# Two of four token tiles take their layer-norm sums on ScalarE, and half of the last stores leave from its queue

## The chip, the cores and the metric

The kernel runs on one core of a Trainium2 chip. The metric is the device time of one execution in microseconds (us), as the median of several runs. The engines are TensorE (PE in the profile; PEld is its weight load), VectorE (DVE), ScalarE (ACT), GpSimd (POOL) and SyncE (SP), which only issues DMAs. Each engine works through its own queue in the order in which the program was laid out, and waits on semaphores for the others.

## The reference

Two transformer blocks run one after the other on 512 tokens of width 1024, in float32. The first has a hybrid mixer, a cross-attention over 256 memory tokens and a mixture of 16 experts; the second is modulated by a conditioning vector and has a Hyena mixer (FFT-like long convolutions) and an expert-choice mixture of 16 experts. What matters here is the layer norm that stands between the stages:

```python
def layer_norm(x, g, b):
    xf = x.astype(jnp.float32)
    mu = xf.mean(-1, keepdims=True)
    var = jnp.square(xf - mu).mean(-1, keepdims=True)
    return ((xf - mu) * lax.rsqrt(var + LN_EPS) * g + b).astype(x.dtype)
...
x = _ln_affine(DEEPNORM_ALPHA_2 * x + (1.0 + m_l[2]) * yl, ln_g[i, 0], ln_b[i, 0])
hl = _modulate(x, m_l[3], m_l[4])
x = _ln_affine(DEEPNORM_ALPHA_2 * x + (1.0 + m_l[5]) * _expert_choice_moe(hl, moe_router[i], moe_w1[i], moe_w3[i], moe_w2[i]),
               ln_g[i, 1], ln_b[i, 1])
```

`_modulate` is a second layer norm (without its own g and b) that is scaled and shifted by modulation rows, so a token tile goes through two norms in a row before it enters the next stage. The last norm gives the output.

## The kernel before, in words

The 512 tokens lie as four **tiles** of 128 tokens (partitions) by 1024 features. The text calls them tile 0 to tile 3; `xr[:, j]` is the residual stream of tile j. The norms are computed at these three places, which the change touches:

- **First norms** (`combine`, L1282 to L1305, at 758 to 808 us): after the first expert mixture. Per tile one add (L1283), a norm in place on `xr` with the position table `pe` added (`ln_affine`), then a norm into a separate tile `mo` (`ln_modulate`). PE transposes `mo` (L360), ACT copies the result out as the high half `hlh` (L235) and DVE subtracts for the low half `hll` (L236). Between them stand ACT's copies of `pe` (L1265) and the splitting of the first Hyena weights (`wh`, L228 on ACT and L231 on DVE). PE starts the first Hyena products on tiles 0 and 1 (`hyena_first`) while tiles 2 and 3 are still in their norms, and finishes them when those are there.
- **Second norms** (`route2`, L1549 to L1555, at 1081 to 1129 us): after the Hyena mixer. Per tile two halves of the product are scaled (L1552) and added (L1553), then normed in place on `xr`, then normed into `hl`, from which the router's affinities come. Tile 0's second norm is spread already: its sums are on ACT (`ln_stats_act`, L327 and L330), its affine part on ACT (L350) and POOL (L351, L352).
- **Last norms** (`moe2`, L1767 to L1782, at 2074 us to the end): on the sums in PSUM (`pcb`), in halves of 512. Tiles 0 and 1 get their affine part on ACT (L1776), DVE (L1777) and POOL (L1778), tiles 2 and 3 on DVE alone (L1780, L1781). Eight stores of 256 KB go out from SP's queue (L1782).

On DVE the statistics are two `bn_stats` on halves of 512 (L316), one `bn_aggr` (L318) and an add of epsilon (L320). Then POOL takes the power -0.5 (`ly`, L308), while DVE does (r - mu) * g (L339), which doesn't need `ly`. When `ly` is there, DVE does the second step, times `ly` plus b (L340).

The order of instructions on each engine is set by the tile framework's scheduler from the order of the calls, the data dependencies and the `issue_after` marks, and is fixed when the program is built. Between the second and the last norms lies the second expert mixture: SP streams all its weights (some 190 loads of 2 MB) through eight slots of SBUF, from 1079 us on, and PE works them off.

Of the kernel before, what the change touches and what calls it, by code (L numbers as in the profile page):

```python
# [13 lines left out]
AF = mybir.ActivationFunctionType  # L14
ALU = mybir.AluOpType
# [4 lines left out]
P = 128  # L20
S = 512
D = 1024
# [181 lines left out]
class Builder:  # L204
# [129 lines left out]

    def ln_affine(self, r, eps, g, b, out=None):
        vec = self.nc.vector
        mu, rs = self.ln_stats(r, eps)
        out = r if out is None else out
        vec.scalar_tensor_tensor(out, r, mu, g, op0=ALU.subtract, op1=ALU.mult)  # L339
        return vec.scalar_tensor_tensor(out, out, rs, b, op0=ALU.mult, op1=ALU.add)  # L340

    def ln_modulate(self, r, sc, sh, out, spread=False):

        if not spread:
            return self.ln_affine(r, 1e-6, sc, sh, out=out)
        nc = self.nc
        mu, rs = self.ln_stats_act(r, 1e-6, out)
        nm = self.small([P, 1], "nmr")
        nc.vector.scalar_tensor_tensor(nm, mu, -1.0, rs, op0=ALU.mult, op1=ALU.mult)
        nc.scalar.activation(out, r, AF.Identity, bias=nm, scale=rs)  # L350
        nc.gpsimd.tensor_tensor(out, out, sc, op=ALU.mult)  # L351
        return nc.gpsimd.tensor_tensor(out, out, sh, op=ALU.add)  # L352
# [896 lines left out]
    def combine(self, xr, ig, tables):  # L1249
# [32 lines left out]
        def norms(j):  # L1282
            vec.tensor_tensor(xr[:, j], xr[:, j], ys[:, j], op=ALU.add)  # L1283
            last.append(self.ln_affine(xr[:, j], 1e-5, g, pe[:, j]))
            mo = self.wide(name="mo")
            last.append(self.ln_modulate(xr[:, j], sc, sh, mo))
            return mo
# [228 lines left out]
    def route2(self, xr, z2, w):  # L1516
# [32 lines left out]
        def norms(j):  # L1549
            for n in range(2):  # L1550
                c = slice(n * 512, (n + 1) * 512)
                tt(hl[:, j, c], pbs[j][n], g2[:, c], op=ALU.mult)  # L1552
                tt(xr[:, j, c], xr[:, j, c], hl[:, j, c], op=ALU.add)  # L1553
            self.ln_affine(xr[:, j], 1e-5, g, b)
            self.ln_modulate(xr[:, j], sc, sh, hl[:, j], j == 0)  # L1555

# [64 lines left out]
    def moe2(self, xr, hl, sv, aff):  # L1621
# [145 lines left out]
        for j in range(4):  # L1767
            mu, rs = self.ln_stats(pbs[j], 1e-5)
            if j < 2:
                nm = self.small([P, 1], "nmr")  # L1770
                vec.scalar_tensor_tensor(nm, mu, -1.0, rs, op0=ALU.mult, op1=ALU.mult)
            for h in range(2):
                c = slice(h * 512, (h + 1) * 512)
                o = xr[:, j, c]
                if j < 2:
                    act.activation(o, pbs[j][h], AF.Identity, bias=nm, scale=rs)  # L1776
                    tt(o, o, gb[0][:, c], op=ALU.mult)  # L1777
                    pool.tensor_tensor(o, o, gb[1][:, c], op=ALU.add)  # L1778
                else:
                    vec.scalar_tensor_tensor(o, pbs[j][h], mu, gb[0][:, c], op0=ALU.subtract, op1=ALU.mult)  # L1780
                    vec.scalar_tensor_tensor(o, o, rs, gb[1][:, c], op0=ALU.mult, op1=ALU.add)  # L1781
                nc.sync.dma_start(self.out[:, j, c], o)  # L1782

# [17 lines left out]
```

## Time and profile before

| | us |
|---|---|
| runs | 2095.79, 2084.8, 2096.02; median 2095.79 |
| profiled execution, time | 2096.14 |
| its span in the profile | 2094.4 |

| engine | busy us | share of the span |
|---|---|---|
| PE | 1854.0 | 89% |
| DVE | 944.2 | 45% |
| ACT | 536.8 | 26% |
| POOL | 186.3 | 9% |

The shares are means over stages with different limits. In the first half DVE and ACT are busy at 3 to 8 tenths, in the second half, the last expert mixture, at 0 to 2 tenths, while the DMA engines move 427 GB/s. A row of the timeline gives start, duration, engine, line, operation, output and input tiles with their shapes, and in brackets how long the engine stood idle before it and what ended that. SPq and ACTq are the DMA issues of those queues.

### The profile page before, as it was taken

To read this page: it belongs to the slowest core of one execution; us is meant where nothing else is said; L and a number is where in the kernel's file an instruction comes from. 1 tells how busy PE (TensorE), PEld (TensorE's weight loads), DVE (VectorE), ACT (ScalarE), POOL (GpSimd) and SP (SyncE) were. 2 spreads that over 40 slices of the span, in tenths; PEclk is the share of its full clock that TensorE was granted. 3 is DMA by queue.
4 is the path that set the end of the run, shared out by engine and by line. 5 is a ranking of instruction groups with operands and counts; after the bars stand their busy time and mean duration, and the time that the engine had idled before them with its cause. 6 is when DMAs were issued, how large, how long until landed. Compare 5 with 4: busy or idle time off the path is not lost.

```text
span 2094.4 us, 21241 instructions
## 1 busy us (share of the span) xinstructions
PE 1854.0 (89%) x8380; PEld 1043.7 (50%) x8380; DVE 944.2 (45%) x1465; ACT 536.8 (26%) x752; POOL 186.3 (9%) x157
## 2 busy tenths in 40 slices
PE   7999799988589869998887999998999889898996
PEld 4777578756456638786764333332333333232332
DVE  7878777664655548549988102020201111020203
ACT  6555333342255524433322100000000000000000
POOL 0000200001101021005551000000000000000001
PEclk9999999998799969999998999999999999999998
DMA  5454277762689852222237799999999999999995
GB/s 167 161 165 167 101 251 252 254 234 72 222 317 372 295 149 97 78 88 97 95 144 318 330 429 427 429 427 424 427 427 428 428 427 428 427 428 428 428 428 224
DMA packets 85551, 601.49 MB, mean 287 GB/s; under 512 B 11598, under 2 KB 13094, under 8 KB 57798
## 3 DMA queue, kind: packets, MB, share of 16 engines
q1 hardware_dynamic: 77270, 575.67, 69.3%
q0 software_dynamic: 3888, 13.57, 2.0%
q10 hardware_dynamic: 4288, 10.85, 1.3%
q8 instruction: 67, 1.10, 0.2%
q14 instruction: 38, 0.31, 0.0%
HBM read 578.00 MB, written 22.05 MB: 286 GB/s over the span
## 4 chain that ended last, share of the span: by engine, by line
PE 41%; DMA 16%; DVE 8%; issue 3%; ACT 2%; POOL 2%; DVEq 0%; SPq 0%; ACTq 0%; POOLq 0%
PE py L1747 11%; DMA ra<-in_w 8%; PE pc L1713 6%; PE pa L1713 6%; DMA r<-in_w 5%; PE pga L1678 3%; DMA wg<-in_wgu 2%; PE pye L222 2%; PE pcb L1764 2%; PE phy L218 2%; PE phy L220 2%; PE phy L219 2%; POOL ly L308 1%; DVE lst L316 1%; DVE wh L231 1%
## 5 line engine op out<-in xcount | busy, mean ns | idle before, releaser
L1717 DVE TENSOR_TENSOR he<-he,pc 128x512 f32<-128x512 f32 x32 | 22.0, 688 | 467.0 <-PE pc L1713 442.8
L1713 PE MATMUL pa<-ra,xe 128*64 128x512 f32 x768 | 178.5, 595 | 9.1 <-DMA ra<-in_w 8.5
L231 DVE TENSOR_TENSOR wh<-w,wh 128x1024 fp32r<-128x1024 f32 x124 | 151.4, 1237 | 36.3 <-ACT wh L228 34.9
L1747 PE MATMUL py<-ra,ht 128*64 128x512 f32 x640 | 150.3, 599 | 0.0
L228 ACT ACTIVATE wh<-w 128x1024 fp32r<-128x1024 f32 x124 | 128.9, 1057 | 80.8 <-DMA w<-in_wmix 12.9
L308 POOL TENSOR_TENSOR ly<-lve,mhalf 128x1 f32<-128x1 f32 x28 | 36.2, 1294 | 1187.3 <-DVE lve L320 1182.5
L1716 ACT ACTIVATE he<-pa 128x512 f32<-128x512 f32 x32 | 19.1, 597 | 461.0 <-PE pa L1713 461.0
L1713 PE MATMUL pc<-r,xe 128*64 128x512 f32 x512 | 119.0, 602 | 16.9 <-DMA r<-in_w 16.9
L1753 DVE TENSOR_TENSOR y<-py,m 64x512 f32<-64x512 f32 x32 | 22.0, 689 | 247.0 <-PE py L1747 246.6
L1713 PE MATMUL pc<-ra,xe 128*64 128x512 f32 x512 | 114.5, 594 | 15.4 <-DMA ra<-in_w 15.4
L1713 PEld LDWEIGHTS pa<-ra,xe 128*64 128x64 f32 x768 | 58.5, 137 | 115.3 <-issue 94.0
L1721 ACT ACTIVATE ht<-pht 128x512 f32<-128x512 f32 x32 | 19.1, 597 | 294.3 <-PE pht L1720 294.3
L1747 PE MATMUL py<-r,ht 128*64 128x512 f32 x376 | 92.1, 595 | 0.7 <-DMA r<-in_w 0.7
L1747 PEld LDWEIGHTS py<-ra,ht 128*64 128x64 f32 x640 | 47.7, 138 | 90.2 <-issue 89.9
L218 PE MATMUL phy<-hlh,wh 128*128 128x512 f32 (+1 forms) x240 | 87.1, 367 | 1.4 <-ACT cv L1379 1.4
L219 PE MATMUL phy<-hll,wh 128*128 128x512 f32 (+1 forms) x240 | 86.5, 361 | 0.4 <-DVE hll L236 0.4
L220 PE MATMUL phy<-hlh,wh 128*128 128x512 f32 (+1 forms) x240 | 86.5, 361 | 0.0
L1713 PEld LDWEIGHTS pc<-r,xe 128*64 128x64 f32 x512 | 38.6, 138 | 94.2 <-issue 74.0
L1713 PEld LDWEIGHTS pc<-ra,xe 128*64 128x64 f32 x512 | 36.8, 137 | 91.3 <-issue 78.8
L222 PE MATMUL pye<-wd,ht 128*128 128x512 f32 x128 | 60.9, 618 | 11.3 <-ACT ht L1139 11.3
L1764 PE MATMUL pcb<-y,ct 128*128 128x512 f32 x128 | 57.2, 598 | 6.5 <-DVE y L1753 6.5
L1423 POOL TENSOR_TENSOR sp<-sp,sp 128x512 f32<-128x512 f32 x32 | 46.8, 1482 | 175.8 <-DVE sp L1422 175.6
(538 smaller groups left out, 3675.6 us busy)
## 6 DMA issues: line engine op xcount, KB each, us to landing
ra<-in_w SPq DMA_DIRECT2D x120, 2048.0 KB
r<-in_w SPq DMA_DIRECT2D x70, 2048.0 KB
wm<-in_modw SPq DMA_DIRECT2D x48, 512.0 KB
w<-in_wgu SPq DMA_DIRECT2D x36, 512.0 KB
wd<-in_wd SPq DMA_DIRECT2D x16, 1024.0 KB
wg<-in_wgu SPq DMA_DIRECT2D x7, 2048.0 KB
w<-in_wpair SPq DMA_DIRECT2D x20, 512.0 KB
w<-in_wh SPq DMA_DIRECT2D x20, 512.0 KB
```

Of the source, the lines that this page charges most:

```text
L218: te.matmul(ps, a.h, b.h, start=first, stop=False, skip_group_check=skip)
L219: te.matmul(ps, a.h, b.l, start=False, stop=False, skip_group_check=skip)
L220: self.lastmm = te.matmul(ps, a.l, b.h, start=False, stop=last, skip_group_check=skip)
L222: te.matmul(ps, a, b, start=first, stop=last, skip_group_check=skip)
L228: nc.scalar.activation(d.h, f, AF.Copy)
L231: (lo_eng or nc.vector).tensor_tensor(d.l, f, d.h.bitcast(F32), op=ALU.subtract)
L308: self.lastpow = self.nc.gpsimd.tensor_tensor(y, v, self.mhalf[:, :n], op=ALU.pow)
L1423: pool.tensor_tensor(t[2 * i], t[2 * i], t[2 * i + 1], op=op)
L1678: te.matmul(p[h * NS:(h + 1) * NS], oh[:, j], hl[:, j, h * 512:(h + 1) * 512], start=j == 0, stop=j == 3)
L1713: te.matmul(p[g * NS:(g + 1) * NS], xs[:, 4 * kh + k], w(k, g), start=kh + k == 0, stop=kh + k == 4)
L1747: te.matmul(py[o:o + NS], ht[:, 4 * hh + i, g * NS:(g + 1) * NS], w(i, n), start=c + i == 0, stop=c + i == 6)
L1764: te.matmul(pb[n], cts[n][:, j * P:(j + 1) * P], yts[n], start=e < E - 1, stop=True)
```

## The change

At the first and second norms tiles 1 and 2 take the sums of both norms on ACT (`ln_stats_act`): a Copy with a running sum, then a Square with minus the mean as bias and a running sum, with an unused tile (`ys` or `hl`) as the throw-away output. At the last norms tiles 1 and 3 take their sums on ACT in halves (`ln_stats_halves`, new), with `ht` as throw-away output. There tile 1's add of b moves from POOL to DVE, and the second half of each tile's store is issued from ACT's queue. Lines of the changed kernel are 19 higher than before in the shared helpers (L339 is L358 there, L340 is L359), 21 to 24 higher at the end.

```diff
+    def ln_stats_halves(self, r, eps, junk):
+
+        act, vec = self.nc.scalar, self.nc.vector
+        s = self.small([P, 4], "lsa", bufs=2).rearrange("p (i h) -> p i h", i=2)
+        m = self.small([P, 2], "lmv")
+        for i, f in enumerate((AF.Copy, AF.Square)):
+            for h in range(2):
+                kw = dict(bias=m[:, 1:2]) if i else {}
+                act.activation(junk[:, h * 512:(h + 1) * 512], r[h], f, accum_out=s[:, i, h:h + 1], **kw)
+            t = self.small([P, 1], "lve")
+            vec.tensor_tensor(t, s[:, i, 0:1], s[:, i, 1:2], op=ALU.add)
+            if i == 0:
+                vec.tensor_scalar(m[:, 0:1], t, 1.0 / D, None, op0=ALU.mult)
+                vec.tensor_scalar(m[:, 1:2], t, -1.0 / D, None, op0=ALU.mult)
+        ve = self.small([P, 1], "lve")
+        vec.tensor_scalar(ve, t, 1.0 / D, eps, op0=ALU.mult, op1=ALU.add)
+        return m[:, 0:1], self.rsqrt(ve, 1, "l")
+
+    def ln_affine(self, r, eps, g, b, out=None, junk=None):
+
         vec = self.nc.vector
-        mu, rs = self.ln_stats(r, eps)
+        mu, rs = self.ln_stats(r, eps) if junk is None else self.ln_stats_act(r, eps, junk)
...
-            return self.ln_affine(r, 1e-6, sc, sh, out=out)
+            return self.ln_affine(r, 1e-6, sc, sh, out=out, junk=junk)
...
-            last.append(self.ln_affine(xr[:, j], 1e-5, g, pe[:, j]))
+            junk = ys[:, j] if j in (1, 2) else None
+            last.append(self.ln_affine(xr[:, j], 1e-5, g, pe[:, j], junk=junk))
             mo = self.wide(name="mo")
-            last.append(self.ln_modulate(xr[:, j], sc, sh, mo))
+            last.append(self.ln_modulate(xr[:, j], sc, sh, mo, junk=junk))
...
-            self.ln_affine(xr[:, j], 1e-5, g, b)
-            self.ln_modulate(xr[:, j], sc, sh, hl[:, j], j == 0)
+            junk = hl[:, j] if j in (1, 2) else None
+            self.ln_affine(xr[:, j], 1e-5, g, b, junk=junk)
+            self.ln_modulate(xr[:, j], sc, sh, hl[:, j], j == 0, junk=junk)
...
-            mu, rs = self.ln_stats(pbs[j], 1e-5)
+            if j % 2:
+                mu, rs = self.ln_stats_halves(pbs[j], 1e-5, htb)
+            else:
+                mu, rs = self.ln_stats(pbs[j], 1e-5)
...
-                    pool.tensor_tensor(o, o, gb[1][:, c], op=ALU.add)
+                    (pool if j == 0 else vec).tensor_tensor(o, o, gb[1][:, c], op=ALU.add)
...
-                nc.sync.dma_start(self.out[:, j, c], o)
+                (nc.sync, nc.scalar)[h].dma_start(self.out[:, j, c], o)
```

The helper that the first and second norms now call stands in the kernel before (L323 to L333). In the orders below a tile's name carries its number, which is the same in both kernels.

First norms, ACT before, from the copies of `pe` on (`pt_6881` and `pt_6888` are tile 1's transposes; `w_6914` is the sixth Hyena weight):

```order
L1265 ACTIVATE pe_6779<-prw_6873 128x1024
L1265 ACTIVATE pe_6779<-prw_6877 128x1024
L235 ACTIVATE hlh_6809<-pt_6881 128x4x128
L235 ACTIVATE hlh_6809<-pt_6888 128x4x128
L228 ACTIVATE wh_6905<-w_6899 128x1024
L228 ACTIVATE wh_6908<-w_6901 128x1024
L228 ACTIVATE wh_6911<-w_6903 128x1024
L246 DMA w_6914<-in_wh 128x1024
L228 ACTIVATE wh_6916<-w_6914 128x1024
```

ACT in the changed kernel, from the same copies on (`lsa_6848` are the sums of tile 1's second norm, `lsa_7064` those of tile 2's first):

```order
L1284 ACTIVATE pe_6779<-prw_6873 128x1024
L1284 ACTIVATE pe_6779<-prw_6877 128x1024
L327 ACTIVATE ys_6800,lsa_6848<-xr_1989 128x1024
L330 ACTIVATE ys_6800,lsa_6848<-xr_1989,lsa_6848 128x1024
L327 ACTIVATE ys_6800,lsa_7064<-xr_1989 128x1024
L235 ACTIVATE hlh_6809<-pt_6881 128x4x128
L235 ACTIVATE hlh_6809<-pt_6888 128x4x128
L228 ACTIVATE wh_6905<-w_6899 128x1024
L228 ACTIVATE wh_6908<-w_6901 128x1024
L228 ACTIVATE wh_6911<-w_6903 128x1024
L246 DMA w_6914<-in_wh 128x1024
L330 ACTIVATE ys_6800,lsa_7064<-xr_1989,lsa_7064 128x1024
```

The sums of tile 1's second norm stand behind both copies of `pe`, the first sum of tile 2 stands ahead of the copies of tile 1's transposes, and its second sum behind three weight splits and a DMA issue.

First norms, DVE before, at tile 3's second norm (`pt_7111` is the first transpose of tile 2):

```order
L316 BN_STATS lst_7100<-xr_1989 128x6 x2
L318 BN_AGGR lmv_7103<-lst_7100 128x2
L320 TENSOR_SCALAR lve_7105<-lmv_7103 128x1
L339 SCALAR_TENSOR_TENSOR mo_7099<-xr_1989,lmv_7103,rows3_6778 128x1024
L236 TENSOR_TENSOR hll_6810<-pt_7111,hlh_6809 128x4x128
L340 SCALAR_TENSOR_TENSOR mo_7099<-mo_7099,ly_7107,rows3_6778 128x1024
```

DVE in the changed kernel at the same norm:

```order
L316 BN_STATS lst_7100<-xr_1989 128x6 x2
L318 BN_AGGR lmv_7103<-lst_7100 128x2
L236 TENSOR_TENSOR hll_6810<-pt_7111,hlh_6809 128x4x128
L320 TENSOR_SCALAR lve_7105<-lmv_7103 128x1
L358 SCALAR_TENSOR_TENSOR mo_7099<-xr_1989,lmv_7103,rows3_6778 128x1024
L236 TENSOR_TENSOR hll_6810<-pt_7118,hlh_6809 128x4x128
L359 SCALAR_TENSOR_TENSOR mo_7099<-mo_7099,ly_7107,rows3_6778 128x1024
```

The low half of tile 2's transpose, which waits for PE and ACT, now stands ahead of `lve_7105`, on which tile 3's second norm rests.

Second norms, POOL before (`ly_9289` belongs to tile 1's first norm, `hl2` with L351 and L352 to tile 0's second):

```order
L308 TENSOR_TENSOR ly_9211<-lve_9209,mhalf_76 128x1
L308 TENSOR_TENSOR ly_9222<-lve_9220,mhalf_76 128x1
L308 TENSOR_TENSOR ly_9289<-lve_9287,mhalf_76 128x1
L351 TENSOR_TENSOR hl2_9088<-hl2_9088,row_9083 128x1024
L352 TENSOR_TENSOR hl2_9088<-hl2_9088,row_9085 128x1024
L308 TENSOR_TENSOR ly_9300<-lve_9298,mhalf_76 128x1
```

POOL in the changed kernel:

```order
L308 TENSOR_TENSOR ly_9211<-lve_9209,mhalf_76 128x1
L308 TENSOR_TENSOR ly_9222<-lve_9220,mhalf_76 128x1
L370 TENSOR_TENSOR hl2_9088<-hl2_9088,row_9083 128x1024
L371 TENSOR_TENSOR hl2_9088<-hl2_9088,row_9085 128x1024
L308 TENSOR_TENSOR ly_9289<-lve_9287,mhalf_76 128x1
L308 TENSOR_TENSOR ly_9300<-lve_9298,mhalf_76 128x1
```

The power for tile 1's first norm moved behind the two steps of 1024 on tile 0's `hl2`.

Last norms, ACT before, to the end of the program (`pcb_12393` is tile 0's sum, `pcb_12394` tile 1's):

```order
L1721 ACTIVATE ht_9616<-pht_12339 128x512
L1716 ACTIVATE he_12383<-pa_12345 128x512
L1721 ACTIVATE ht_9616<-pht_12386 128x512
L1776 ACTIVATE xr_1989<-pcb_12393,nmr_12463,ly_12461 128x512 x2
L1776 ACTIVATE xr_1989<-pcb_12394,nmr_12482,ly_12480 128x512 x2
```

ACT in the changed kernel, from the last norms to the end (`pcb_12397` and `pcb_12398` are the halves of tile 3):

```order
L343 ACTIVATE ht_9616,lsa_12473<-pcb_12394 128x512
L1800 ACTIVATE xr_1989<-pcb_12393,nmr_12463,ly_12461 128x512 x2
L343 ACTIVATE ht_9616,lsa_12473<-pcb_12394 128x512
L1806 DMA out_0<-xr_1989 128x512
L343 ACTIVATE ht_9616,lsa_12473<-pcb_12394,lmv_12474 128x512 x2
L343 ACTIVATE ht_9616,lsa_12514<-pcb_12397 128x512
L343 ACTIVATE ht_9616,lsa_12514<-pcb_12398 128x512
L1800 ACTIVATE xr_1989<-pcb_12394,nmr_12489,ly_12487 128x512 x2
L1806 DMA out_0<-xr_1989 128x512 x2
L343 ACTIVATE ht_9616,lsa_12514<-pcb_12397,lmv_12515 128x512
L343 ACTIVATE ht_9616,lsa_12514<-pcb_12398,lmv_12515 128x512
L1806 DMA out_0<-xr_1989 128x512
```

Between the first and the second sums of tile 1 now stands the issue of tile 0's second half, and ahead of tile 3's second sums stand two more issues.

## Rows read from the trace of the kernel before

**Rows 1.** Busy time by stretch, with the view's own column heads.

```profile
core 0: us, PE busy (x) PEld busy (x) DVE busy (x) ACT busy (x) POOL busy (x), PEclk, DMA share, GB/s
770.00:782.50 12.50, 9.82 (x22) 4.95 (x20) 11.44 (x18) 3.84 (x5) 2.92 (x2) 0.50 0.22 72
861.00:914.00 53.00, 53.00 (x244) 43.09 (x244) 25.36 (x48) 23.88 (x35) 0.00 (x0) 1.00 0.27 83
1086.00:1091.00 5.00, 5.00 (x24) 4.14 (x23) 4.90 (x8) 0.39 (x1) 1.52 (x1) 1.00 0.28 116
1156.00:1161.00 5.00, 3.56 (x20) 1.32 (x18) 0.43 (x1) 1.19 (x2) 0.00 (x0) 1.00 0.00 0
1204.00:1500.00 296.00, 277.29 (x1220) 96.16 (x1218) 41.84 (x75) 19.96 (x32) 0.00 (x0) 0.99 1.01 427
```

**Rows 2.** Timeline: tile 1's second norm on DVE, at the first norms.

```profile
775.93 1.29 DVE L316 BATCH_NORM_STATS2 lst<-xr 128x6 f32<-128x512 f32 x2
777.25 0.21 DVE L318 BATCH_NORM_AGGREGATE lmv<-lst 128x2 f32<-128x12 f32 x1
777.50 0.15 DVE L320 TENSOR_SCALAR lve<-lmv 128x1 f32<-128x1 f32 x1
777.58 1.28 DVE L339 SCALAR_TENSOR_TENSOR mo<-xr,lmv,rows 128x1024 f32<-128x1024 f32 x1
777.80 1.47 POOL L308 TENSOR_TENSOR ly<-lve,mhalf 128x1 f32<-128x1 f32 x1 [3.22 <-DVE lve L320]
779.30 1.28 DVE L340 SCALAR_TENSOR_TENSOR mo<-mo,ly,rows 128x1024 f32<-128x1024 f32 x1 [0.44 <-POOL ly L308]
```

**Rows 3.** Timeline of ACT, second norms: tile 0's sums on ACT.

```profile
1090.61 1.06 ACT L327 ACTIVATE hl<-xr 128x1024 f32<-128x1024 f32 x1 [16.86 <-DVE xr L340]
1092.11 1.16 ACT L330 ACTIVATE hl<-xr,lsa 128x1024 f32<-128x1024 f32 x1 [0.34 <-DVE lsa L329]
1093.16 0.18 ACT L330 ACTIVATION_READ_ACCUMULATOR hl<-xr,lsa 128x1 f32 x1
```

**Rows 4.** Timeline, first norms: ACT's other work, transposes, tile 3's last step.

```profile
778.09 1.02 ACT L1265 ACTIVATE pe<-prw 128x1024 f32<-128x1024 f32 x1 [2.39 <-PE prw L1264]
783.21 2.94 ACT L228 ACTIVATE wh<-w 128x1024 fp32r<-128x1024 f32 x3
789.20 1.06 ACT L228 ACTIVATE wh<-w 128x1024 fp32r<-128x1024 f32 x1 [3.06 <-DMA w<-in_wh]
803.22 1.04 PE L360 MATMUL pt<-c_ident,mo 128*128 128x128 f32 x8
804.56 0.68 DVE L236 TENSOR_TENSOR hll<-pt,hlh 128x512 fp32r<-128x512 f32 x1
805.16 1.28 DVE L340 SCALAR_TENSOR_TENSOR mo<-mo,ly,rows 128x1024 f32<-128x1024 f32 x1
```

**Rows 5.** Timeline, second norms: POOL on tile 0, DVE on tile 1.

```profile
1096.32 2.40 POOL L351 TENSOR_TENSOR hl<-hl,row 128x1024 f32<-128x1024 f32 x1
1098.80 3.26 POOL L352 TENSOR_TENSOR hl<-hl,row 128x1024 f32<-128x1024 f32 x1
1096.39 3.42 DVE L340 SCALAR_TENSOR_TENSOR xr<-xr,ly,rows 128x1024 f32<-128x1024 f32 x1 [0.44 <-POOL ly L308]
1127.63 1.29 DVE L340 SCALAR_TENSOR_TENSOR hl<-hl,ly,row 128x1024 f32<-128x1024 f32 x1 [0.37 <-POOL ly L308]
```

**Rows 6.** Timeline of the last norms, then the stores' group.

```profile
2078.94 2.86 POOL L1778 TENSOR_TENSOR xr<-xr,gb 128x512 f32<-128x512 f32 x2 [2.07 <-DVE xr L1777]
2081.77 0.54 POOL L308 TENSOR_TENSOR ly<-lve,mhalf 128x1 f32<-128x1 f32 x1
2082.54 1.45 ACT L1776 ACTIVATE xr<-pcb,nmr,ly 128x512 f32<-128x512 f32 x2 [4.00 <-DVE nmr L1771]
2089.74 1.40 DVE L1781 SCALAR_TENSOR_TENSOR xr<-xr,ly,gb 128x512 f32<-128x512 f32 x2
L1782 SPq DMA_DIRECT2D out<-xr x8: 332/338/398, 2080.6 to 2091.2; - x8
```

More of the change, by code (lines that the diff above doesn't have):

```diff
@@ L333, in ln_stats_act @@
         return s[:, 1:2], self.rsqrt(ve, 1, "l")
-    def ln_affine(self, r, eps, g, b, out=None):
+    def ln_stats_halves(self, r, eps, junk):
[15 more added lines that the diff above has]
+    def ln_affine(self, r, eps, g, b, out=None, junk=None):
         vec = self.nc.vector
-        mu, rs = self.ln_stats(r, eps)
+        mu, rs = self.ln_stats(r, eps) if junk is None else self.ln_stats_act(r, eps, junk)
         out = r if out is None else out
@@ L340, in ln_affine, with ln_modulate @@
         return vec.scalar_tensor_tensor(out, out, rs, b, op0=ALU.mult, op1=ALU.add)
-    def ln_modulate(self, r, sc, sh, out, spread=False):
+    def ln_modulate(self, r, sc, sh, out, spread=False, junk=None):
         if not spread:
-            return self.ln_affine(r, 1e-6, sc, sh, out=out)
+            return self.ln_affine(r, 1e-6, sc, sh, out=out, junk=junk)
         nc = self.nc
```

## The prediction

> **What bounds the kernel now.** I read the busy time by stretch first. From 861 to 914 us PE is busy for the whole 53.00 us: the Hyena mixer starts when the first norms hand over their tiles and then runs on PE without a gap [rows 1]. From 1086 to 1091 us, in the second norms, DVE is busy for 4.90 of 5 us and ACT for 0.39: DVE sets the pace there and ACT is free [rows 1]. From 1156 to 1161 us no weights move, because the slots are full and wait for the first expert; from 1204 us on the DMA share is 1.01 [rows 1]. So the weight stream limits the last 900 us, but when it resumes depends on when the norms end. I read from this that a microsecond won or lost at any of the three places moves the end by one.
>
> **One norm, both ways.** In the timeline, tile 1's second norm has its input at 775.93 and begins its last step at 779.30: 3.37 us. DVE's two statistics take 1.29, and the power on POOL (1.47) runs beside DVE's first step (1.28) [rows 2]. The sums on ACT of tile 0 in the trace run from 1090.61 until the second accumulator read ends at 1093.34: 2.73 us, with DVE's division between them [rows 3]. Then 0.2 for epsilon. If DVE's first step must still follow, with the power beside it, 1.72 more pass (777.58 to 779.30 [rows 2]): 4.65, or **1.3 us longer** than on DVE. It must follow where it writes what Square still reads or writes: in place on `xr` at the first norm of a tile, and on `hl` at the second norms. Only with `mo` (first norms) does it run beside Square; the power alone then follows, between 0.54 [rows 6] and 1.47 [rows 2], and the norm takes 3.5 to 4.4.
>
> What is saved is DVE time: per norm the statistics and the aggregate, 1.29 + 0.21 [rows 2], less two small divisions of about 0.1 each: 1.3 us, over eight norms 10.4 us. It only counts if DVE has other work ready in its order.
>
> **First norms: +6 us.** In tile 1's second norm the Copy stands behind the two copies of `pe`, and the second of these runs from 778.09 to 779.11, since it waits for PE [rows 4]. The sum thus begins at 779.1 and not at 775.93. With 2.73, 0.2 and a power of 0.6 the last step begins at 782.7 instead of 779.30: +3.4. Next, ACT's order puts tile 2's Copy (1.06 + 0.18 as in [rows 3]) ahead of the `hlh` copies of tile 1, with which PE's first Hyena products begin: +4.5 for PE. Tile 2's Square then waits behind three weight splits (2.94 [rows 4]) and the issue of the sixth weight; that weight's split comes at 789.20 now [rows 4] and moves by as much, and with it the add of tile 3, which DVE now has behind it. By this chain alone tile 3 is 4.5 us late. But DVE's order also puts the `hll` of tile 2 ahead of the `lve` of tile 3's second norm. That `hll` follows tile 2's transposes, which PE reaches at 803.22 now, after the first products [rows 4]; late by 4.5 they come at 807.7, `hll` starts 1.34 later (803.22 to 804.56 [rows 4]) and takes 0.68, so `lve` runs at 809.7 and the last step at 811.0 to 811.6. Before it began at 805.16 [rows 4]: about **+6**. Bounds: 0, if PE's backlog covered all of it, and 9, if every one of the four norms' 1.3 us came on top of the 3.4.
>
> **Second norms: +3.8 us.** On POOL the power of tile 1's first norm moved behind two steps on tile 0's `hl`. These took 2.40 and 3.26, from 1096.32 to 1102.06; beside them DVE's last step of tile 1 took 3.42 instead of 1.28 and ended at 1099.81 [rows 5]. In the new order the two steps come first, uncontended 2.40 each, from about 1095.9 to 1100.7, then the power (0.55), then the last step: it ends at 1102.6, +2.8. Tile 1's second norm adds 1.3 (+4.1). Tile 2's scaled halves now run partly inside these waits and give back 1.2 (+2.9); its own two norms add 2.6 (+5.5); tile 3's four halves (2.4 us of DVE) run inside their waits, and 0.7 of that is lost again to ACT, where two router copies stand ahead of tile 2's last Square. That leaves tile 3 late by some **3.8**. Its norms are on DVE as before, so its last step begins at about 1131.4 instead of 1127.63 [rows 5]. Bounds: 0, if all gaps were filled, and 7.
>
> **Last norms: +3.1 us.** ACT's order puts the store of tile 0's second half between the first and the second sums of tile 1. That store waits for POOL's adds, which run from 2078.94 to 2081.80 [rows 6]. The Squares thus start at 2081.9. Half of a Square of 1024 is 0.58 [rows 3], half of two affine steps is 0.73 [rows 6]; with an accumulator read of 0.18 [rows 3] behind each half, partly hidden, I take 0.78 for each. The power that before ran at 2081.77 [rows 6] comes at 2083.85, and tile 1's affine part, at 2082.54 before [rows 6], at 2084.85: +2.3. Tile 3's Squares wait behind two more issues, the last of which follows tile 1's elementwise work on DVE. Four steps of about 0.7 (half of 1.40 [rows 6]), two of them the adds that came from POOL, stand there behind the two last steps of tile 2, and end at 2089.2; with the issue the Squares end at 2091.2. After that come epsilon, power, and two last steps of 0.7: DVE ends at 2094.2 instead of 2091.14 (2089.74 + 1.40 [rows 6]). Bounds: 0 and 5. Splitting the stores over two queues I cost at nothing: SP's eight issues take 0.338 each [rows 6], and the last follows the last step either way. The Trainium skill ("DMA: Bandwidth & Descriptors", Issuing engines are not separate DMA queues) says that several issuing engines only save the time of issuing; by that rule the split could win at most 4 x 0.338 = 1.35 us, and the sum would be 11.5 instead of 12.9; the trace speaks for nothing won, because SP is busy for only 2.7 us between 2080.6 and 2091.2.
>
> **Sum.** 6 + 3.8 + 3.1 = 12.9 us on the profiled execution's 2096.14: **2109**. The profiled time is 0.35 above the median of the runs, 2095.79, so the sum stands to the median the same way. The bounds add up to 0 and +21.
>
> **Rivals.**
> *DVE's saving wins (2084).* At the second norms DVE is at 4.90 of 5 us with ACT free [rows 1]; if its freed 1.3 us per norm are filled with the next tile's work, four norms there and four at the first place give 10.4 us back, and the last norms about 1.5. This decides where a tile's Copy starts as soon as its input is there and the next tile's adds stand in DVE's order before the Square's result. For it speaks DVE's load; against it, that in both orders little work of the next tile stands there.
> *PE covers the first norms (2103).* PE works on the first products until tile 2's transposes at 803.22 [rows 4]; if these start on time, because ACT serves `hlh` sooner than I think, tile 3's delay shrinks to nothing and only 6.9 us are left. Against it: the Copy stands ahead of `hlh` in ACT's order.
> *A longer wait costs clock too (2116).* From 770 to 782.5 us, in the first norms, PE has gaps (9.82 of 12.5 us busy) and the granted clock is 0.50, the 1.2 GHz level; from 861 us on it is 1.00, 2.4 GHz [rows 1]. If PE's longer idle time before tile 3 brings the low level back, and the next 7 us of its work run there, that costs 3.5 us more at each of the two places. Against it: the first products run up to tile 2's transposes in both orders.
> *The sums don't reach ACT as cheaply as the rows show*: a table load at each switch between Copy and Square would make them dearer than in [rows 3]. The orders show no load on these pieces of ACT's queue, so I give this no time and no chance of its own.
>
> **Chances.** Forecast 0.60 (2101 to 2115), PE covers 0.17, DVE's saving 0.13, clock 0.10. About 1% (21 us, 2075 to 2117) is what a measurement of this kernel can tell from no change. DVE's saving reaches past 1% only in its tail (0.03), the clock case for more than half of its chance (0.07); the rest, 0.90, lies within. The range goes from 2087, near the saving's 2084, to 2117, which takes in most of the clock case and the upper bound of the sum.
>
> **What would show it.** Right: the last step of tile 3 at the first norms begins near 811 and at the second norms near 1137 (3.8 plus the 6 carried over), the weight stream stands still longer, tile 1's power at the last norms comes two microseconds later after PE's end. Wrong: DVE's gaps at the norms don't grow, ACT's Copy starts with its input, or the stretch from 861 us on takes the delay up. A change of more than 21 us in either direction would say that a place I did not price has moved.

## The result, and the profile after

The changed kernel takes 2103.6 us (median of 8 runs, 2095.7 to 2108.4) against 2090.19 for the kernel before in the same comparison (8 runs, 2082.6 to 2096.0). The ratio is 1.0055, with a 95% interval of 1.0039 to 1.0072: 8 to 15 us slower, less than 1%. The profiled execution took 2106.41 us with a span of 2104.7. DVE is busy for 930.6 us (944.2 before), ACT for 559.8 (536.8), POOL for 180.4 (186.3): the work moved as intended, and the time went up.

The kernel before takes anything from 2081.4 to 2101.0 us in the 105 runs taken beside the experiments, so I read each place by itself, from start to start in the timeline. Of the kernel before, these are the first adds of the first and of the second norms and PE's first product into the last sums:

```profile
758.52 1.23 DVE L1283 TENSOR_TENSOR xr<-xr,ys 128x1024 f32<-128x1024 f32 x1 [22.15 <-DMA ys<-yd,ig]
1082.21 2.15 DVE L1553 TENSOR_TENSOR xr<-xr,hl 128x512 f32<-128x512 f32 x1
2072.40 5.42 PE L1764 MATMUL pcb<-y,ct 128*128 128x512 f32 x12 [0.80 <-DVE y L1753]
```

The ends of its three stretches stand in [rows 4 to 6]. Of the changed kernel, the same points and the ends:

```profile
759.39 1.22 DVE L1302 TENSOR_TENSOR xr<-xr,ys 128x1024 f32<-128x1024 f32 x1 [22.11 <-DMA ys<-yd,ig]
810.53 1.28 DVE L359 SCALAR_TENSOR_TENSOR mo<-mo,ly,rows 128x1024 f32<-128x1024 f32 x1
1086.08 2.15 DVE L1573 TENSOR_TENSOR xr<-xr,hl 128x512 f32<-128x512 f32 x1
1137.98 1.29 DVE L359 SCALAR_TENSOR_TENSOR hl<-hl,ly,row 128x1024 f32<-128x1024 f32 x1 [0.37 <-POOL ly L308]
2079.74 5.42 PE L1785 MATMUL pcb<-y,ct 128*128 128x512 f32 x12 [0.80 <-DVE y L1774]
2100.01 1.42 DVE L1805 SCALAR_TENSOR_TENSOR xr<-xr,ly,gb 128x512 f32<-128x512 f32 x2 [0.73 <-POOL ly L308]
```

| stretch (us) | before | after | term of the prediction | in traces where that place is unchanged |
|---|---|---|---|---|
| first norms: first add to tile 3's last step | 46.64 | 51.14 | +6 | 46.63 to 46.65 in nine, 47.77 in one |
| from there to the second norms | 277.05 | 275.55 | 0 | 272.4 to 277.5 |
| second norms: first add to tile 3's last step | 45.42 | 51.90 | +3.8 | 45.4 to 46.9 in nine, median 46.26 |
| from there to PE's first product into the last sums | 944.77 | 941.76 | 0 | 941.5 to 944.8 |
| last norms: from that product to DVE's end | 18.74 | 21.69 | +3.1 | 18.73 or 18.74 in nine |

The traces of the last column are those of the experiments below and of the kernel before; for the last norms experiment 9, where only the stores differ, is among the nine. The first and the last place hold to a few hundredths of a microsecond (one trace aside), the second to 1.5 us. The stretches between them scatter by 3 to 5 us whatever the kernel is, and the first add itself comes anywhere from 751.3 to 760.6 us, ahead of everything that was changed: that is the noise of the totals. Behind a longer place the next stretch is no shorter (275.2 to 276.8 and 941.8 to 944.2 us, within the last column), so neither takes up a delay. Measured against the last column the places are 4.5, 5.6 and 3.0 us longer, together 13.1; the medians differ by 13.4.

**First norms, after.** The timeline in order of the chain; the first row is the last step of tile 1's first norm, the second answers to the copy of `pe` in [rows 4], the last three to its transposes and low half; tile 3's last step (810.53) is the second row of the fence above.

```profile
775.90 1.28 DVE L359 SCALAR_TENSOR_TENSOR xr<-xr,ly,pe 128x1024 f32<-128x1024 f32 x1
778.96 1.02 ACT L1284 ACTIVATE pe<-prw 128x1024 f32<-128x1024 f32 x1 [2.39 <-PE prw L1283]
779.88 1.05 ACT L327 ACTIVATE ys<-xr 128x1024 f32<-128x1024 f32 x1
783.51 1.28 DVE L359 SCALAR_TENSOR_TENSOR mo<-mo,ly,rows 128x1024 f32<-128x1024 f32 x1 [0.73 <-POOL ly L308]
785.96 1.06 ACT L327 ACTIVATE ys<-xr 128x1024 f32<-128x1024 f32 x1 [3.37 <-DVE xr L1302]
787.02 1.06 ACT L235 ACTIVATE hlh<-pt 128x512 fp32r<-128x512 f32 x2
787.65 0.80 PE L218 MATMUL phy<-hlh,wh 128*128 128x256 f32 x2 [0.76 <-ACT hlh L235]
806.80 1.04 PE L379 MATMUL pt<-c_ident,mo 128*128 128x128 f32 x8
808.07 0.69 DVE L236 TENSOR_TENSOR hll<-pt,hlh 128x512 fp32r<-128x512 f32 x1 [1.47 <-ACT hlh L235]
808.67 0.14 DVE L320 TENSOR_SCALAR lve<-lmv 128x1 f32<-128x1 f32 x1
```

The input of tile 1's second norm is there at 777.18 (775.90 + 1.28), but its sum starts 2.70 us later, right behind the second copy of `pe`; tile 1's last step comes 24.12 us after the first add instead of 20.78, 3.34 late. Tile 2's Copy stands ahead of the copies of the transposes, which adds 0.93: PE's first product waits for ACT and starts at +28.26 instead of +23.99. The low half of tile 2 follows its transposes, and tile 3's addition of epsilon follows the low half: from there to the last step (810.53) it is 2.46 us, where it was 0.60 [rows 4].

**Second norms, after.** ACT, POOL and DVE, the part that answers to [rows 5]:

```profile
1097.92 1.05 ACT L327 ACTIVATE hl<-xr 128x1024 f32<-128x1024 f32 x1
1099.12 1.25 ACT L369 ACTIVATE hl<-xr,nmr,ly 128x1024 f32<-128x1024 f32 x1
1100.44 2.40 POOL L370 TENSOR_TENSOR hl<-hl,row 128x1024 f32<-128x1024 f32 x1 [1.61 <-ACT hl L369]
1102.92 3.26 POOL L371 TENSOR_TENSOR hl<-hl,row 128x1024 f32<-128x1024 f32 x1
1106.14 0.55 POOL L308 TENSOR_TENSOR ly<-lve,mhalf 128x1 f32<-128x1 f32 x1
1101.60 2.33 DVE L358 SCALAR_TENSOR_TENSOR xr<-xr,lsa,rows 128x1024 f32<-128x1024 f32 x1
1106.73 1.29 DVE L359 SCALAR_TENSOR_TENSOR xr<-xr,ly,rows 128x1024 f32<-128x1024 f32 x1 [2.80 <-POOL ly L308]
1126.51 0.17 DVE L1591 TENSOR_REDUCE rmx<-plt 128x1 f32<-128x16 f32 x1 [1.98 <-PE plt L222]
1126.60 0.14 DVE L332 TENSOR_SCALAR lve<-lsa 128x1 f32<-128x1 f32 x1
1135.87 0.17 DVE L1591 TENSOR_REDUCE rmx<-plt 128x1 f32<-128x16 f32 x1 [1.31 <-PE plt L222]
```

Tile 1's Copy now runs ahead of ACT's affine step on tile 0 (1099.12), POOL's two steps follow that step and take 2.40 and 3.26 as before, and the power (1106.14) waits behind them, so DVE sits idle for 2.80 us ahead of the last step of tile 1's first norm ("<-POOL ly"). Behind most sums on ACT DVE waits again, for 0.8 to 2.2 us each. Later, the addition of epsilon of tile 2's second norm (1126.60) stands behind a reduction of the router (`rmx`, one for each tile), for which DVE waited 1.98 us. And right ahead of the aggregate of tile 3's second norm DVE waits once more, 1.31 us for the reduction of tile 2 (1135.87); in the kernel before that reduction comes at 1125.48 without a wait.

**Last norms, after** (answers to [rows 6]; ACTq is the issue of a store from ACT's queue):

```profile
2086.01 2.93 POOL L1802 TENSOR_TENSOR xr<-xr,gb 128x512 f32<-128x512 f32 x2 [1.81 <-DVE xr L1801]
2088.97 0.35 ACTq L1806 DMA_DIRECT2D out<-xr  x1
2089.42 0.69 ACT L343 ACTIVATE ht<-pcb,lmv 128x512 f32<-128x512 f32 x1 [2.97 <-POOL xr L1802]
2093.94 2.88 ACTq L1806 DMA_DIRECT2D out<-xr  x2
2096.36 0.15 DVE L348 TENSOR_SCALAR lmv<-lve 128x1 f32<-128x1 f32 x1
2096.92 0.69 ACT L343 ACTIVATE ht<-pcb,lmv 128x512 f32<-128x512 f32 x1 [3.30 <-DVE lmv L348]
```

The Squares of tile 1 begin right after the issue, and the issue right after POOL's adds end (2088.94). The Squares of tile 3 (2096.92) wait for two things that end almost together: the mean (2096.36 + 0.15), which stands behind tile 1's steps on DVE, and the two issues ahead of them in ACT's queue, the second of which ends at 2096.82.

### The profile page after: what moved, and what is told of

Its sections match the earlier page's. It is cut to its first block, busy times and chain, and to the rows that moved or that the text cites. A ratio compares the mean times of both kernels' runs of the same rounds, so it can differ in the third digit from the quotient of the medians.

```text
span 2104.7 us, 21300 instructions
## 1 busy us (share of the span) xinstructions
PE 1857.7 (88%) x8380; PEld 1045.2 (50%) x8380; DVE 930.6 (44%) x1461; ACT 559.8 (27%) x800; POOL 180.4 (9%) x155
## 4 chain that ended last, share of the span: by engine, by line
PE 41%; DMA 17%; DVE 7%; issue 3%; ACT 3%; POOL 2%; SPq 0%; ACTq 0%; DVEq 0%; POOLq 0%
PE py L1768 11%; DMA ra<-in_w 8%; PE pc L1734 6%; PE pa L1734 6%; DMA r<-in_w 5%; DMA wg<-in_wgu 3%; PE pga L1699 3%; PE phy L218 2%; PE phy L219 2%; PE phy L220 2%; PE pcb L1785 2%; PE pye L222 2%; DVE he L1738 1%; PE pht L1741 1%; DVE wh L1449 1%
## 5 line engine op out<-in xcount | busy, mean ns | idle before, releaser
L1443 POOL TENSOR_TENSOR sp<-sp,sp 128x512 f32<-128x512 f32 x32 | 46.9, 1484 | 176.0 <-DVE sp L1442 175.8
```

Source lines behind the costliest of these rows:

```text
L1443: pool.tensor_tensor(t[2 * i], t[2 * i], t[2 * i + 1], op=op)
```

## The experiments

Each kernel was run 12 times beside 35 runs of the kernel before. No single place changes the time by much more than its interval, so each was also read by its stretch. "Before" means the order or the engine of the kernel before.

| | what is changed | ratio (95%) | its stretch, us |
|---|---|---|---|
| 1 | first norms | 1.0032 (1.0017 to 1.0048) | 52.04 |
| 2 | second norms | 1.0040 (1.0023 to 1.0058) | 51.78 |
| 3 | last norms | 1.0016 (0.9997 to 1.0035) | 21.70 |
| 4 | first norms, tile 1's second norm on DVE | 1.0004 (0.9986 to 1.0021) | 48.79 |
| 5 | as 4, epsilon ahead of the low half | 1.0003 (0.9985 to 1.0022) | 47.57 |
| 6 | second norms, POOL's order as before | 1.0017 (1.0002 to 1.0032) | 49.89 |
| 7 | second norms, tile 1 alone | 1.0020 (1.0004 to 1.0037) | 48.41 |
| 8 | second norms, tile 2 alone | 1.0007 (0.9989 to 1.0025) | 48.21 |
| 9 | only the stores split | 1.0003 (0.9990 to 1.0017) | 18.73 |
| 10 | last norms, stores on SP | 1.0016 (1.0001 to 1.0031) | 20.51 |
| 11 | last norms, tile 3's sums alone | 1.0008 (0.9997 to 1.0020) | 20.94 |
| 12 | as 11, tile 3's mean ahead | 1.0001 (0.9981 to 1.0021) | 19.67 |

**1 to 3: one place at a time.** Edits to the changed kernel. The other two places are as before; for the last norms (in 1 and 2) that takes three more lines, which are left out here:

```diff
-            junk = ys[:, j] if j in (1, 2) else None   # out in 2 and 3
+            junk = None
-            junk = hl[:, j] if j in (1, 2) else None   # out in 1 and 3
+            junk = None
```

> Only the first norms take their sums on ScalarE; second and last norms and the stores are as before. In the changed kernel the stretch from the first add to the start of tile 3's last step grew from 46.6 to 51.1 us (+4.5). Theory A (each place loses on its own and hands its loss on): 51.1 us here too, the second and last norms at 45.4 and 18.7 us as before, and the time +3 to +5 us. Theory B (the loss of a place depends on the others, or a later stage takes it up): 51.1 us here, but the time within 1 us of before.

> Only the second norms take their sums on ScalarE. In the changed kernel the stretch from the first add to the start of tile 3's last step grew from 45.4 to 51.9 us (+6.5). Theory A: 51.9 us here, the time +4 to +7 us. Theory B: the stretch grows, but the weight stream of the last expert mixture takes it up and the time stays within 2 us.

> Only the last norms and the stores are changed (sums of tiles 1 and 3 on ScalarE, one add moved from GpSimd to VectorE, second halves stored from ScalarE's queue). In the changed kernel the stretch from the first pcb matmul to the end of VectorE's last step grew from 18.7 to 21.7 us (+3.0). Nothing comes behind it, so theory A and theory B both say +3 us in the time; a time of +1 or less would say that the stretch is not what sets the end.

Every place alone is slower or level, none is faster. The stretches are those of the whole change (52.04, 51.78, 21.70 against 51.14, 51.90, 21.69), so each place loses on its own and hands its loss on, theory A. The 0.9 us by which the first norms are longer in 1 than in the whole change are explained in the third section. The single ratios add up to 0.88% against 0.55% for the whole; within their intervals the two agree.

**4: first norms, tile 1's second norm on DVE.** Edit to 1:

```diff
-            last.append(self.ln_modulate(xr[:, j], sc, sh, mo, junk=junk))
+            last.append(self.ln_modulate(xr[:, j], sc, sh, mo, junk=junk if j == 2 else None))
```

> First norms only, as in the change, but tile 1's second norm keeps its statistics on DVE, so that its sum does not stand behind the copies of the position table on ACT. The stretch from the first add to tile 3's last step was 46.6 us before and 52.0 with all four norms of tiles 1 and 2 on ACT. Theory (the wait behind the copies is passed on through the copy of the transposes and PE's first products): 48 to 49.5. Rival (each norm's own 1.3 us counts, whichever it is): about 50.7. Other rival (tile 2's sums behind the weight splits set tile 3 alone): stays at 51.5 to 52.

48.79: 3.25 of the 5.4 us go. The edit takes away the wait behind the copies of `pe` and the sum's own length together; by the rows of the changed kernel the wait is 2.70 us of tile 1's delay, and from its start on ACT the norm is only 0.26 longer than on DVE (3.63 against 3.37 [rows 2]). Of tile 3's second norm, DVE in this kernel:

```profile
795.59 0.21 DVE L318 BATCH_NORM_AGGREGATE lmv<-lst 128x2 f32<-128x12 f32 x1
797.59 0.69 DVE L236 TENSOR_TENSOR hll<-pt,hlh 128x512 fp32r<-128x512 f32 x1 [1.80 <-ACT hlh L235]
798.20 0.14 DVE L320 TENSOR_SCALAR lve<-lmv 128x1 f32<-128x1 f32 x1
800.05 1.28 DVE L359 SCALAR_TENSOR_TENSOR mo<-mo,ly,rows 128x1024 f32<-128x1024 f32 x1
```

The low half (797.59) comes 46.33 us after the first add (751.26 here), as good as before (46.04); but the addition of epsilon, whose input was ready at 795.8, waits behind it, and the last step comes 2.46 us after the low half.

**5: epsilon ahead of the low half again.** Edit to 4 (`lastve` is the last addition of epsilon):

```diff
-        self.transpose_rows(m2, 2, hl)
+        with self.tc.issue_after(self.lastve.ins):
+            self.transpose_rows(m2, 2, hl)
```

> First norms only, tile 1's second norm on DVE as in the run before that gave 48.8 us, and now also DVE's low half of tile 2's transposes put behind tile 3's addition of epsilon again, as it stood in the kernel before. In that run the low half came 46.3 us after the first add (46.0 in the kernel before), but the addition of epsilon stood behind it and the last step 2.4 us after that. Theory (this order alone makes the 2.2 us that are left): 46.8 to 47.3. Rival (tile 3 is late by its own input, since tile 2's sums hold DVE): 48 to 48.8.

47.57: nearer to the theory than to the rival, but just above its range. From the low half to the last step it is 0.61 again, so this order was worth 1.85 us, as [rows 4] had it. The stretch is only 1.22 shorter, because the low half itself came at 46.96 here instead of 46.33. PE started its first products at the same point in both (+25.33 and +25.32), but the level of 1.2 GHz lasted for 6.5 us behind that here and 5.4 in experiment 4; the third section has more on it.

**6: second norms, POOL's order as before.** Edit to 2: the two steps on tile 0 are called behind the power of tile 1's first norm.

```diff
+            if j == 1:
+                with self.tc.issue_after(self.lastpow.ins):
+                    self.rest()          # L370, L371
```

> As the run with the second norms alone, but the two GpSimd steps on tile 0's hl are called behind tile 1's first norm, which puts tile 1's power back ahead of them in GpSimd's queue, where it stood before. Theory of the queue (the wait of 2.8 us for the power behind those two steps is the largest single loss): tile 1's last step of its first norm starts 3 to 4 us sooner, and the stretch is 47.5 to 50 us instead of 51.9. Theory of the sums (ScalarE's sums are 1.3 us longer per norm, and that is the loss): the stretch stays within 1 us of 51.9.

The last step of tile 1's first norm starts 3.83 us sooner than in experiment 2 (+16.58 against +20.41 after the first add), but it then runs beside POOL's first step again and takes 3.42 us instead of 1.28. Net, POOL's order costs 1.9 us: part of the loss, and neither theory's whole.

```profile
1096.56 3.42 DVE L359 SCALAR_TENSOR_TENSOR xr<-xr,ly,rows 128x1024 f32<-128x1024 f32 x1 [0.44 <-POOL ly L308]
```

**7 and 8: second norms, one tile each.** Edit to 2; 8 has POOL's order of the kernel before, 7 that of the change.

```diff
-            junk = hl[:, j] if j in (1, 2) else None
+            junk = hl[:, j] if j == 1 else None      # in 8: j == 2
```

> Second norms only, and there only tile 1's sums on ACT; the power of tile 1's first norm stands behind POOL's two steps on tile 0, as in the change. Where this place is as before, the stretch from its first add to tile 3's last step was 45.4 to 46.9 us (seven kernels, median 46.3); with tiles 1 and 2 on ACT 51.8, and with the old order on POOL 49.9. Theory A (the costs add: POOL's order 1.9, tile 1's two norms 1.3 each): 50 to 51, and tile 2's part is small. Theory B (tile 1's lateness is partly taken up by the gaps of tile 2's norms, which are on DVE here): 48 to 49.5.

> Second norms only, and there only tile 2's sums on ACT; tile 1 and POOL's order are as before. Theory A (tile 2's two norms cost their own 1.3 us each, and the step of its second norm that stands behind the router's reduction on DVE another 2): 48 to 50. Theory B (the loss is tile 1's and POOL's, and tile 2's sums are hidden beside the router's work): 46 to 47.

Tile 1 with POOL's order costs 2.15 us (48.41 - 46.26), theory B; tile 2 costs 1.95 (48.21), theory A by its number but only half by its reason. Its two norms do come 1.34 us later each. But tile 2's second norm does not stand behind the router's reduction in 8: its last step comes at 1116.50, ahead of the first reduction, for which DVE then waits only 0.21 us. In 2, where both tiles are moved, that wait is 2.10, and tile 2's second norm stands behind it. The first two rows are of 8, the last two of 2, each time the first reduction and the one ahead of tile 3's aggregate:

```profile
1118.58 0.17 DVE L1591 TENSOR_REDUCE rmx<-plt 128x1 f32<-128x16 f32 x1 [0.21 <-PE plt L222]
1126.91 0.15 DVE L1591 TENSOR_REDUCE rmx<-plt 128x1 f32<-128x16 f32 x1
```

```profile
1118.65 0.18 DVE L1591 TENSOR_REDUCE rmx<-plt 128x1 f32<-128x16 f32 x1 [2.10 <-PE plt L222]
1128.01 0.17 DVE L1591 TENSOR_REDUCE rmx<-plt 128x1 f32<-128x16 f32 x1 [1.31 <-PE plt L222]
```

These make 4.1, and both tiles together cost 5.5. The traces show where the missing 1.4 arise. Up to the last step of tile 3's first norm the costs do add: 4.2 us late in 2, 2.3 in 7 and 2.1 in 8, against the median of the nine. From there to tile 3's last step it is 4.79 to 4.83 us in the nine, 4.66 in 7 and 4.68 in 8, but 6.17 in 2, 6.18 in 6 and 6.17 in the whole change. In that stretch lies the second wait, 1.31 us right ahead of tile 3's aggregate, for the router's reduction of tile 2, whose second norm is that late only when both tiles are moved. So the 1.4 fit this wait, and the earlier one of 2.10 counts by making tile 2 late. Neither was taken out by itself.

**9: only the stores split.** Sums and adds as before.

```diff
-                nc.sync.dma_start(self.out[:, j, c], o)
+                (nc.sync, nc.scalar)[h].dma_start(self.out[:, j, c], o)
```

> The kernel before with only the store split: the second half of each tile goes out from ACT's queue. Theory (the prediction's, splitting costs and wins nothing by itself): the last stretch stays at 18.7 us, the time from DVE's end to the end of the span at 3.3, and the time within 0.15%. Rival (two queues save issuing time): the end comes up to 1.4 us sooner. Other rival (the issue for tile 0 on ACT holds tile 1's affine part, which stands behind it): the last stretch gets longer by more than 0.5 us.

18.73, and 3.25 from DVE's end to the end of the span (3.26 before): nothing won, nothing lost, as the prediction had it. The Trainium skill ("DMA: Bandwidth & Descriptors", Issuing engines are not separate DMA queues) left room for 1.35 us of issuing time; by this run none of it shows.

**10: last norms, all stores on SP.** The edit of 9 undone in 3.

> The kernel before with the last norms' sums of tiles 1 and 3 on ACT and tile 1's adds on DVE, as in the change, but with all eight stores issued from SP's queue. Theory (the stores in ACT's queue hold the second sums): in the changed kernel tile 1's Squares stood behind the issue of tile 0's second half, which waited for POOL's adds. Without the issue they start about 2.5 us sooner, and the stretch from PE's start on the last sums in PSUM to DVE's end, 18.7 us before and 21.7 with the whole change at this place, falls to 19 to 20. Rival (the sums' own length and the round trips between ACT and DVE make the loss): it stays at 21 to 21.7. Time within 0.3% of the kernel before under both.

20.51, between the two: the issues in ACT's queue are worth 1.2 of the 3.0 us. Tile 1's Squares start 8.83 us after PE's first product instead of 9.68, so 0.85 sooner and not the 2.5 that were expected, for they still wait for their mean, and tile 3's are held as in the whole change:

```profile
2074.44 1.22 DVE L345 TENSOR_TENSOR lve<-lsa 128x1 f32<-128x1 f32 x1
2076.48 0.69 ACT L343 ACTIVATE ht<-pcb,lmv 128x512 f32<-128x512 f32 x1 [2.10 <-DVE lmv L348]
2083.66 0.69 ACT L343 ACTIVATE ht<-pcb,lmv 128x512 f32<-128x512 f32 x1 [2.99 <-DVE lmv L348]
```

The add of two accumulators (L345, one column) takes 1.22 us beside POOL's adds, and the mean of tile 3 (at 2083.42) comes behind tile 1's adds on DVE. The other 1.8 us thus lie between DVE and ACT; how they divide over DVE's order, tile 1's adds there and the handovers was not taken apart.

**11: last norms, tile 3's sums alone on ACT.** Adds on POOL and stores on SP as before.

```diff
-            if j % 2:
+            if j == 3:
                 mu, rs = self.ln_stats_halves(pbs[j], 1e-5, htb)
```

> Last norms only, and there only tile 3's sums on ACT; tile 1's sums, the adds on POOL and the stores on SP are as before. Theory (work that DVE loses is a gain where ACT is free in time and no store stands ahead): DVE's statistics of tile 3, 1.3 us, are gone, its two halves follow those of tile 2 without a gap, and the last stretch is 17.3 to 18.0 us instead of 18.7. Rival (the handovers between ACT and DVE, about 1.2 us each, eat it): 18.7 to 20. The time itself moves by less than 0.1% either way.

20.94: both were wrong. Nothing stood ahead on ACT, and it still cost 2.2 us. DVE, POOL and ACT show two reasons:

```profile
2080.45 3.31 POOL L1802 TENSOR_TENSOR xr<-xr,gb 128x512 f32<-128x512 f32 x2 [1.30 <-DVE xr L1801]
2080.89 3.42 DVE L1805 SCALAR_TENSOR_TENSOR xr<-xr,ly,gb 128x512 f32<-128x512 f32 x2
2084.23 0.15 DVE L345 TENSOR_TENSOR lve<-lsa 128x1 f32<-128x1 f32 x1
2084.72 0.69 ACT L343 ACTIVATE ht<-pcb,lmv 128x512 f32<-128x512 f32 x1 [4.85 <-DVE lmv L348]
```

DVE's two last steps of tile 2 take 3.42, beside POOL's adds of tile 1; the same two steps took 2.73 in the kernel before, and two such steps alone take 1.40 [rows 6]. And tile 3's mean stands behind them, so ACT's Squares begin at 2084.72, though the sums had been there since 2077.1.

**12: tile 3's mean ahead of tile 2's last steps.** Edit to 11: tile 3's statistics are called right behind tile 2's.

```diff
+            if j == 2:
+                mr3 = self.ln_stats_halves(pbs[3], 1e-5, htb)
+            if j == 3:
+                mu, rs = mr3
```

> Last norms only, tile 3's sums alone on ACT as in the run that gave 20.9 us, but its statistics are called ahead of tile 2's elementwise steps, so that DVE forms the mean and ACT the second sums while DVE works on tile 2. Theory (the loss was the mean standing behind tile 2's last steps on DVE, which made tile 3 wait 2.2 us in two gaps, 0.9 and 0.7, and its first steps start late): 18.0 to 18.9, that is level with the 18.7 of the kernel before or a little under it. Rival (DVE's last steps, slowed beside POOL's adds of tile 1, set the end, whatever the order): 19.5 to 21.

19.67, in the rival's range: the order is worth 1.3 us, and DVE's two steps beside POOL still take 3.30:

```profile
2077.26 3.31 POOL L1804 TENSOR_TENSOR xr<-xr,gb 128x512 f32<-128x512 f32 x2 [1.37 <-DVE xr L1803]
2077.83 3.30 DVE L1807 SCALAR_TENSOR_TENSOR xr<-xr,ly,gb 128x512 f32<-128x512 f32 x2
```

The kernel before, too, has them beside POOL's adds (3.31 from 2084.57), but there they are apart, with another step and an aggregate of DVE between them, and lose less:

```profile
2085.01 1.76 DVE L1781 SCALAR_TENSOR_TENSOR xr<-xr,ly,gb 128x512 f32<-128x512 f32 x1
2087.47 0.97 DVE L1781 SCALAR_TENSOR_TENSOR xr<-xr,ly,gb 128x512 f32<-128x512 f32 x1
```

The 0.6 us between 3.30 and 2.73 fit part of the 0.9 that still remain against the kernel before; this was not tried by itself. None of the twelve beats the kernel before.

## Why the prediction was right, and where its sizes were off

The forecast was 12.9 us more than before and the medians differ by 13.4, with the three places at 13.1. The forecast of 2109 us lies 5.4 above the 2103.6 measured because the kernel before, too, has a median of 2090.19 in the larger comparison, 5.6 less than in the three runs that I built on. For the same reason 2103.6 falls on the 2103 of the rival *PE covers the first norms*, whose mechanism did not occur. That 13.4 comes so near to 12.9 is partly luck: the first norms cost 1.5 us less than forecast and the second 1.8 more. The mechanism held in the main. Where a step lands in a queue costs time: 2.70 us for the wait that 4 takes away, 1.85 for the order that 5 puts back, 1.9 in 6 and 1.2 in 10. The sums' own length counts as well, 1.34 us a norm for tile 2 in 8, where 1.3 was said.

- **First norms: +6 predicted, +4.5 measured.** The chain came as it was worked out: tile 1's last step 3.34 us late (3.4 said), PE's first products 4.27 (4.5), the order of low half and epsilon 1.86. What was not foreseen is that PE gave back 1.6 us between its first products and tile 2's transposes (20.71 us before, 19.15 after). The kernel before has a gap of 0.39 us there (its first row below: 2.11 of 2.50 us busy), in which PE waits for DVE's first low half, and the changed kernel has none. Apart from that PE is busy all the time in both, but the granted clock differs. The windows' columns are those of [rows 1]; of the kernel before, then of the changed one, each from the start of the first products:

```profile
782.51:785.01 2.50, 2.11 (x9) 1.82 (x9) 2.45 (x4) 2.30 (x3) 0.00 (x0) 0.50 0.00 0
785.01:787.51 2.50, 2.50 (x14) 2.50 (x14) 2.50 (x3) 1.14 (x2) 0.00 (x0) 0.50 0.31 62
787.51:790.01 2.50, 2.50 (x15) 2.50 (x15) 2.02 (x5) 0.81 (x1) 1.46 (x1) 0.61 0.90 342
```

```profile
787.65:790.15 2.50, 2.50 (x10) 2.28 (x11) 2.36 (x3) 2.50 (x4) 0.00 (x0) 0.50 0.00 0
790.15:792.65 2.50, 2.50 (x17) 2.50 (x16) 2.50 (x5) 1.90 (x3) 0.00 (x0) 0.69 0.41 105
```

  From these rows and rows of 1 us, the level of 1.2 GHz (0.50) lasts for 6.96 us before, 6.57 of them busy, and 4.06 after: 2.5 us less of work at half speed give back 1.25, and the gap gives the 0.39. As to the clock, it is not the change that does this. In the kernels whose first norms are as before it lasts from 3.8 to 7.0 us, and in experiment 1, with the same code here as the whole change, 6.06, with tile 2's transposes 0.9 us later and the stretch 0.9 longer (52.04). Where the place is as before, the low half comes at +46.03 to +46.05 in nine of ten whatever the clock does, since DVE comes to it only then, without a wait; once PE is late, the clock counts. So +6 was worked out from a trace with a late rise of the clock, and +4.5 was measured in one with an early rise; experiment 1, with a late one, measured +5.4. What sets the rise, the runs don't show.
- **Second norms: +3.8 predicted, 5.6 measured** (6.5 against the one trace that I had, which lies at the low end of the nine). This term was mis-sized. POOL's pair was taken as 2 x 2.40; it took 2.40 + 3.26 in the new order too, because DVE's first step of tile 1 runs beside it (2.33 instead of 1.28), and it began 0.7 us later than said. Tile 1's Copy, which now runs ahead of ACT's affine step on tile 0, is not the reason for that: the step begins 0.09 us behind the end of its input `nmr` in both kernels. Most of the 0.7 comes from tile 0, which was 0.5 late because DVE waited 0.72 us for PE's product of its second half; two of the nine traces with this place unchanged have such a wait too, so it is not shown to be the change's doing. Together that made tile 1 late by 1.5 us more than said. The larger miss is further on: 0.7 was counted for two router copies on ACT ahead of tile 2's last Square, and nothing for the router's reductions on DVE, where DVE waits 1.98 us inside tile 2's second norm and 1.31 ahead of tile 3's aggregate.
- **Last norms: +3.1 predicted, +2.95 measured.** The points came as worked out, counted from PE's first product: tile 1's Squares at 9.7 (9.5 said), its affine part at 12.4 (12.5), the end of tile 3's Squares at 18.6 (18.8), DVE's end at 21.7 (21.8). One reason was incomplete: tile 3's Squares wait for the mean on DVE (2096.36) as well as for the issues: in experiment 10, without any issue on ACT, ACT still stands idle for 2.99 us ahead of them, for that mean.
- **Stores: 0 predicted, 0 measured** (experiment 9).
- **The rivals.** *DVE's saving wins*: DVE lost 13.6 us of work and every place got longer; even tile 3 alone, with ACT free (11), lost 2.2. *PE covers the first norms*: tile 3 was still 4.5 us late; 1.6 us were covered, by the clock and the gap and not because ACT served `hlh` sooner. *A longer wait costs clock*: not seen at the first norms. Behind tile 3's last step there the level of 1.2 GHz lasts for 3.4 us in both kernels (windows of 1 us), and from 861 to 918 us the granted clock is 1.00 as before. Experiment 1, with the same code there, has 6.8 us of it, and its next stretch, 276.01, is no longer than the others. Around the second norms the level scatters too much to tell, also between kernels in which they are unchanged. *The sums' price on ACT* was as in [rows 3], Copy 1.05 and Square 1.15, with no table load among them. What should show it did: 810.53 (811 said), 1137.98 (1137), of which 0.87 us are the later start of the first add in this trace; tile 1's power at the last norms (2091.39) 11.65 us after PE's first product instead of 9.37; and the weight stream, which stands still for 8 us ahead of tile 3's last step at the second norms instead of 4 (windows of 1 us with a DMA share under 0.1).

## What to carry to other kernels

An engine that is idle on average is no place to put a step for free: ask at which point of its queue the step lands, what stands ahead of it there, and what of the other engines' work then stands behind its result. A sum that goes to another engine and comes back costs two handovers per result, here 1.2 to 1.4 us of idle DVE each where DVE has nothing else ready, against the 1.5 us of statistics that it saves; if it pays, then where the other engine's order already has ready work in between, which no run here shows. Before moving work, look for what a freed slot lets run side by side: here steps of DVE and POOL that slow each other.

## What the hardware showed

DVE's steps with two tensor inputs in SBUF and POOL's do not run beside each other. The step of 1024 takes 1.28 alone and 3.42 when POOL's step of 2.40 began 0.07 us ahead of it [rows 5]; it ends 1.09 us after POOL's end, so it had waited for nearly all of POOL's step. POOL's next step takes 3.26 in turn. A DVE add of two tiles of one column takes 1.22 beside POOL (experiment 10) instead of 0.16. A step with one input is not held: in the kernel before two `bn_stats` of 512 took 1.29 us at 1099.84, as long as elsewhere, beside POOL's second step. The Trainium skill ("SBUF — State Buffer", SBUF: two separate sides) says that the two engines share a pair of ports, which a DVE instruction with two SBUF inputs or a GpSimd one that reads SBUF holds for its whole length while the other is blocked. These rows agree: the steps are paid one after the other, not at a shared rate.

The accumulator read behind each activation takes 0.18 to 0.21 us on ACT, for 512 as for 1024 columns, and a Square of 512 out of PSUM takes 0.69 where the Copy takes 0.59.
